# Row-wise dot products with a softmax on one core: another division of the last step, sums on ScalarE, and a later first store

## The chip, the cores and the metric

One core of one Trainium2 chip. The metric is the device time of a whole execution in microseconds (us); the span is the same execution from its first to its last instruction in the trace, some 1.8 us shorter. In the lines of the profile DVE is VectorE, ACT ScalarE, SP SyncE (which issues the loads); DVEq, ACTq and SPq are the sequencers of these engines.

## The reference

```python
def reference(x, y):                       # x, y: [8, 4096, 512] float32
    gram = np.matmul(x, y.transpose(0, 2, 1))
    diag = np.diagonal(gram, axis1=1, axis2=2)      # [8, 4096]: dot of row n of x with row n of y
    diag = diag - diag.max(axis=-1, keepdims=True)
    exp = np.exp(diag)
    return exp / exp.sum(axis=-1, keepdims=True)
```

Only the diagonal is needed: 32,768 dot products of 512 elements, then a softmax over each 4096. The inputs are 134 MB, the output 0.13 MB.

## The kernel before

The batches go in two sets of four. A set lies on 128 partitions (32 partitions for each batch), with 128 columns of dots for each partition. A set has four steps, and a step takes 32 rows for each partition: 8.39 MB of x and 8.39 MB of y. Six steps multiply the whole tile and reduce it. The last two use one combined multiply-and-sum (a "dot") for each row, and the last one is cut into pieces, so that little is left to do when the last bytes land.

```python
    # ... (views, pools, x in two tiles of 32 rows, y in one)
    def rows(t, r0, n):
        return xs[t % 2][:, r0 : r0 + n, :]

    def dots_of(t, r0, n):
        return diag[t * R // C][:, columns(t, r0, n)]

    def load_x(t, r0, n):
        nc.sync.dma_start(out=rows(t, r0, n), in_=xv[t * R // C, :, columns(t, r0, n), :])

    def load_y(t, r0, n):
        nc.sync.dma_start(out=ys[:, r0 : r0 + n, :], in_=yv[t * R // C, :, columns(t, r0, n), :])

    # ... products: xt = xt * yt on VectorE; sums: a reduce over the columns

    def dots(t, r0, n):
        for r in range(r0, r0 + n):
            xt = xs[t % 2][:, r, :]
            nc.vector.scalar_tensor_tensor(
                out=xt, in0=xt, scalar=1.0, in1=ys[:, r, :], op0=Alu.mult, op1=Alu.mult,
                accum_out=dots_of(t, r, 1),
            )

    # ... over_quadrant: reduces a [P, 1] column over its 32 partitions; largest: maximum over columns

    def exps(i, d):
        mxp = small.tile([P, 1], f32, name=f"mxp{i}")
        largest(mxp, d)
        nmx = over_quadrant(f"nmx{i}", mxp, Alu.max, negate=True)
        sump = small.tile([P, 1], f32, name=f"sump{i}")
        nc.scalar.activation(out=res[i], in_=diag[i][:, :C], func=Act.Exp, bias=nmx, scale=1.0, accum_out=sump)
        return sump

    def store(i, sump, n):
        total = over_quadrant(f"sum{i}", sump, Alu.add)
        rc = small.tile([P, 1], f32, name=f"rc{i}")
        nc.vector.reciprocal(out=rc, in_=total)
        nc.vector.tensor_single_scalar(out=res[i], in_=res[i], scalar=rc, op=Alu.mult)
        for p in range(0, P, n):
            nc.scalar.dma_start(out=ov[i, p : p + n, :], in_=res[i][p : p + n, :])

    for t in range(S - 2):
        load_x(t, 0, R)
        load_y(t, 0, R)
        nc.scalar.activation(out=side, in_=ys[:, R - K :, :], func=Act.Copy)
        products(t, 0, R - K, ys[:, : R - K, :])
        if t == C // R:
            store(0, sump, G)
        products(t, R - K, K, side)
        sums(t, 0, R)
        if t == C // R - 1:
            sump = exps(0, diag[0])

    t = S - 2
    load_x(t, 0, R)
    for r0 in (0, H):
        load_y(t, r0, H)
        dots(t, r0, H)

    t += 1
    r0 = 0
    for n in (16, 8, 4, 2, 1, 1):
        load_x(t, r0, n)
        load_y(t, r0, n)
        if r0 == 0:
            largest(diag[1][:, C : C + 1], diag[1][:, : C - R])
        if r0 == R - 2:
            largest(diag[1][:, C + 1 :], diag[1][:, C - R : C - 2])
        dots(t, r0, n)
        r0 += n
    store(1, exps(1, diag[1][:, C - 2 :]), P)
```

## Time and profile before

| | kernel before |
|---|---|
| time, median of the first 3 runs | 321.35 us (321.05 to 321.68) |
| span of the profiled run | 319.5 us |
| first load issued, last load landed | 0.73, 314.52 us |
| tail's maximum starts, last store issued | 315.35, 317.08 us |
| VectorE, ScalarE busy | 249.1, 18.9 us |

How to read it: the load stream fills the DMA engines from the start to about 313.4 us (busy share 9 tenths or more in 39 of 40 slices of the profile; 385 GB/s from 312 to 313 us, 150 in the microsecond after it and none from 314 to 315). What remains is a short stretch in which VectorE catches up with the last rows, and a serial tail (maximum, exchange over the quadrant, that is the 32 partitions of a batch, exponential, sum, reciprocal, scaling, store). The change works on these last 25 us, apart from the first set's store, which it takes out of the middle. The prediction below shows the lines.

The *first piece's start* is the start of the first VectorE multiplication of the last step. The *tail's maximum* is the first operation of the serial tail, the one whose output the program calls mxp.

### The profile page before, as it was taken

Reading aid. Unit: us, or ns where it says so; the run is one execution under the profiler, and the core shown is the slowest. Engines: PE = TensorE matmul, PEld = TensorE weight load, DVE = VectorE, ACT = ScalarE, POOL = GpSimd, SP = SyncE. Lnnn points to the kernel's source line nnn. Section 1 sums busy time; section 2 is a strip of 40 time slices with the busy share of each in tenths; the row PEclk is TensorE's granted clock in tenths of the full one; section 3 lists DMA queues with packets and bytes.
Section 4 is the critical chain, followed back from the end, with each engine's and each line's share of the span. In section 5 each row is a group of like instructions: output and inputs, shape, how many; then the busy total and the mean of one; then the engine's idle time right before and its main releaser. Section 6 shows DMA issues by size and latency. Waiting matters only on the chain.

```text
span 319.5 us, 284 instructions
## 1 busy us (share of the span) xinstructions
DVE 249.1 (78%) x158; ACT 18.9 (6%) x11; POOL 0.2 (0%) x4
## 2 busy tenths in 40 slices
DVE  0000079996899949999499995999959999994995
ACT  1000030000300003000120003000030000000000
POOL 0000000000000000000000000000000000000000
DMA  9999999999999999999999999999999999999992
GB/s 394 394 394 517 402 394 484 435 394 468 435 410 394 492 427 394 484 435 394 435 476 402 394 509 410 394 492 429 396 414 484 390 419 447 415 431 410 424 411 101
DMA packets 4225, 134.36 MB, mean 421 GB/s; under 512 B 512, under 2 KB 768, under 8 KB 1536
## 3 DMA queue, kind: packets, MB, share of 16 engines
q1 hardware_dynamic: 3888, 134.22, 97.6%
q10 hardware_dynamic: 336, 0.13, 0.1%
q14 instruction: 1, 0.01, 0.0%
HBM read 134.22 MB, written 0.13 MB: 421 GB/s over the span
## 4 chain that ended last, share of the span: by engine, by line
DMA 60%; DVE 36%; issue 2%; SPq 0%; ACT 0%; DVEq 0%
DMA ys<-in_y_dram 60%; DVE xs L69 27%; DVE xs L77 5%; DVE diag L72 4%; SPq L62 0%; DVE res L105 0%; DVE sum L85 0%; DVE nmx L85 0%; ACT res L98 0%; DVE rc L104 0%; DVE mxp L91 0%; SPq L65 0%; DVEq L69 0%; DVEq L77 0%
## 5 line engine op out<-in xcount | busy, mean ns | idle before, releaser
L69 DVE TENSOR_TENSOR xs<-xs,ys 128x13312 f32<-128x13312 f32 x6 | 84.2, 14025 | 62.3 <-DMA ys<-in_y_dram 62.3
L72 DVE TENSOR_REDUCE diag<-xs 128x32 f32<-128x16384 f32 x6 | 103.3, 17220 | 0.2
L77 DVE SCALAR_TENSOR_TENSOR xs<-xs,ys 128x512 f32<-128x512 f32 x64 | 39.6, 685 | 4.6 <-DMA ys<-in_y_dram 4.5
L112 ACT ACTIVATE side<-ys 128x3072 f32<-128x3072 f32 x6 | 16.6, 2765 | 187.5 <-DMA ys<-in_y_dram 151.4
L69 DVE TENSOR_TENSOR xs<-xs,side 128x3072 f32<-128x3072 f32 x6 | 20.1, 3351 | 0.0
L98 ACT ACTIVATE res<-diag,nmx 128x128 f32<-128x128 f32 x2 | 0.8, 402 | 109.2 <-DVE nmx L85 109.2
L77 DVE DVE_READ_ACCUMULATOR xs<-xs,ys 128x1 f32 x64 | 5.2, 81 | 0.0
L112 ACT ACT_TABLE_LOAD x1 | 1.3, 1283 | 0.7 <-PEq L153 0.7
L85 DVE TRANSPOSE_TENSOR_REDUCE sum<-sump 128x1 f32<-128x32 f32 x2 | 0.4, 208 | 0.6 <-ACT res L98 0.6
L105 DVE TENSOR_SCALAR res<-res,rc 128x128 f32<-128x128 f32 x2 | 0.6, 287 | 0.1
L91 DVE TENSOR_REDUCE mxp<-diag 128x1 f32<-128x128 f32 (+1 forms) x2 | 0.4, 222 | 0.1
L91 DVE TENSOR_REDUCE diag<-diag 128x1 f32<-128x96 f32 (+1 forms) x2 | 0.4, 218 | 0.1
L85 DVE TRANSPOSE_TENSOR_REDUCE nmx<-mxp 128x1 f32<-128x32 f32 x2 | 0.4, 212 | 0.1
L104 DVE RECIPROCAL rc<-sum 128x1 f32<-128x1 f32 x2 | 0.3, 164 | 0.1
L98 ACT ACTIVATION_READ_ACCUMULATOR res<-diag,nmx 128x1 f32 x2 | 0.4, 187 | 0.0
L153 POOL MEMSET const-uint8-127<- 128x1 uint8 x1 | 0.1, 103 | 0.0
L153 POOL MEMSET const-bfloat16-1.0<- 128x1 bf16 x1 | 0.1, 102 | 0.0
L153 POOL MEMSET const-float32-0.0<- 128x1 f32 x1 | 0.1, 99 | 0.2 <-issue 0.2
L153 POOL MEMSET const-float32-1.0<- 128x1 f32 x1 | 0.1, 99 | 0.0
## 6 DMA issues: line engine op xcount, KB each, us to landing
ys<-in_y_dram SPq DMA_DIRECT2D x3, 4096.0 KB, 14.9
xs<-in_x_dram SPq DMA_DIRECT2D x1, 4096.0 KB, 14.1
xs<-in_x_dram SPq DMA_DIRECT2D x1, 2048.0 KB, 18.5
ys<-in_y_dram SPq DMA_DIRECT2D x1, 2048.0 KB, 18.9
xs<-in_x_dram SPq DMA_DIRECT2D x1, 1024.0 KB, 21.0
ys<-in_y_dram SPq DMA_DIRECT2D x1, 1024.0 KB, 21.4
xs<-in_x_dram SPq DMA_DIRECT2D x1, 512.0 KB, 22.3
ys<-in_y_dram SPq DMA_DIRECT2D x1, 512.0 KB, 22.8
```

Of the source, the lines that this page charges most:

```text
L69: nc.vector.tensor_tensor(out=xt, in0=xt, in1=yt, op=Alu.mult)
L72: nc.vector.tensor_reduce(out=dots_of(t, r0, n), in_=rows(t, r0, n), axis=X, op=Alu.add)
L77: nc.vector.scalar_tensor_tensor(out=xt, in0=xt, scalar=1.0, in1=ys[:, r, :], op0=Alu.mult, op1=Alu.mult, accum_out=dots_of(t, r, 1),)
L85: nc.vector.tensor_reduce(out=got, in_=column.to_broadcast([P, G]), axis=X, op=op, negate=negate, apply_transpose=True)
L91: nc.vector.tensor_reduce(out=out, in_=d, axis=X, op=Alu.max)
L98: nc.scalar.activation(out=res[i], in_=diag[i][:, :C], func=Act.Exp, bias=nmx, scale=1.0, accum_out=sump)
L104: nc.vector.reciprocal(out=rc, in_=total)
L105: nc.vector.tensor_single_scalar(out=res[i], in_=res[i], scalar=rc, op=Alu.mult)
L112: nc.scalar.activation(out=side, in_=ys[:, R - K :, :], func=Act.Copy)
L153: nc = _bacc.Bacc("TRN2", target_bir_lowering=False, num_devices=1)
```

## The change

The intent is fourfold. The last row is split into two column halves, so that only half a dot follows the last landing. ScalarE sums 12 rows of the first piece, to unload VectorE. The first piece becomes one row larger and the last whole piece two rows. The store of the first set moves from the middle of the load stream to behind the last load.

```diff
 
 
@@ -58,11 +59,11 @@
     def dots_of(t, r0, n):
         return diag[t * R // C][:, columns(t, r0, n)]
 
-    def load_x(t, r0, n):
-        nc.sync.dma_start(out=rows(t, r0, n), in_=xv[t * R // C, :, columns(t, r0, n), :])
+    def load_x(t, r0, n, d=slice(0, D)):
+        nc.sync.dma_start(out=rows(t, r0, n)[:, :, d], in_=xv[t * R // C, :, columns(t, r0, n), d])
 
-    def load_y(t, r0, n):
-        nc.sync.dma_start(out=ys[:, r0 : r0 + n, :], in_=yv[t * R // C, :, columns(t, r0, n), :])
+    def load_y(t, r0, n, d=slice(0, D)):
+        nc.sync.dma_start(out=ys[:, r0 : r0 + n, d], in_=yv[t * R // C, :, columns(t, r0, n), d])
 
     def products(t, r0, n, yt):
         xt = rows(t, r0, n)
@@ -70,6 +71,11 @@
 
     def sums(t, r0, n):
         nc.vector.tensor_reduce(out=dots_of(t, r0, n), in_=rows(t, r0, n), axis=X, op=Alu.add)
+
+    def sums_act(t, r0, n):
+        for r in range(r0, r0 + n):
+            row = xs[t % 2][:, r, :]
+            nc.scalar.activation(out=row, in_=row, func=Act.Copy, accum_out=dots_of(t, r, 1))
 
     def dots(t, r0, n):
         for r in range(r0, r0 + n):
@@ -98,13 +104,11 @@
         nc.scalar.activation(out=res[i], in_=diag[i][:, :C], func=Act.Exp, bias=nmx, scale=1.0, accum_out=sump)
         return sump
 
-    def store(i, sump, n):
+    def normalize(i, sump):
         total = over_quadrant(f"sum{i}", sump, Alu.add)
         rc = small.tile([P, 1], f32, name=f"rc{i}")
         nc.vector.reciprocal(out=rc, in_=total)
         nc.vector.tensor_single_scalar(out=res[i], in_=res[i], scalar=rc, op=Alu.mult)
-        for p in range(0, P, n):
-            nc.scalar.dma_start(out=ov[i, p : p + n, :], in_=res[i][p : p + n, :])
 
     for t in range(S - 2):
         load_x(t, 0, R)
@@ -112,7 +116,7 @@
         nc.scalar.activation(out=side, in_=ys[:, R - K :, :], func=Act.Copy)
         products(t, 0, R - K, ys[:, : R - K, :])
         if t == C // R:
-            store(0, sump, G)
+            normalize(0, sump)
         products(t, R - K, K, side)
         sums(t, 0, R)
         if t == C // R - 1:
@@ -125,17 +129,39 @@
         dots(t, r0, H)
 
     t += 1
+    largest(diag[1][:, C : C + 1], diag[1][:, : C - R])
     r0 = 0
-    for n in (16, 8, 4, 2, 1, 1):
+    for n in (17, 8, 4, 2):
         load_x(t, r0, n)
         load_y(t, r0, n)
         if r0 == 0:
-            largest(diag[1][:, C : C + 1], diag[1][:, : C - R])
-        if r0 == R - 2:
-            largest(diag[1][:, C + 1 :], diag[1][:, C - R : C - 2])
-        dots(t, r0, n)
+            for r in (0, W // 2):
+                products(t, r, W // 2, ys[:, r : r + W // 2, :])
+                sums_act(t, r, W // 2)
+            dots(t, W, n - W)
+        else:
+            dots(t, r0, n)
         r0 += n
-    store(1, exps(1, diag[1][:, C - 2 :]), P)
+
+    left, right = slice(0, D // 2), slice(D // 2, D)
+    for d in (left, right):
+        load_x(t, r0, 1, d)
+        load_y(t, r0, 1, d)
+
+    for p in range(0, P, G):
+        nc.sync.dma_start(out=ov[0, p : p + G, :], in_=res[0][p : p + G, :])
+    largest(diag[1][:, C + 1 :], diag[1][:, C - R : C - 1])
+    part = small.tile([P, 1], f32, name="part")
+    xt, yt = xs[t % 2][:, r0, :], ys[:, r0, :]
+    nc.vector.scalar_tensor_tensor(
+        out=xt[:, left], in0=xt[:, left], scalar=1.0, in1=yt[:, left], op0=Alu.mult, op1=Alu.mult, accum_out=part
+    )
+    nc.vector.tensor_tensor_reduce(
+        out=xt[:, right], in0=xt[:, right], in1=yt[:, right], scale=1.0, scalar=part,
+        op0=Alu.mult, op1=Alu.add, accum_out=dots_of(t, r0, 1),
+    )
+    normalize(1, exps(1, diag[1][:, C - 1 :]))
+    nc.scalar.dma_start(out=ov[1], in_=res[1])
 
 
 # ---- launch: one core; inputs and outputs as the reference has them ----
```

More of the change, by code (lines that the diff above doesn't have):

```diff
@@ L32 @@
     K = 6
+    W = 12
     S = B // Q * (C // R)
```

## The prediction

Sum: -0.15 (earlier landings) + 0.06 (the smaller loads of the last row) - 0.27 (the last dot halved) + 0.4 (VectorE behind), which I put at -0.1 and so at 321.2 us. The term of 0.06: the 314.43 for the right half's landing contains it (314.52 - 0.15 + 0.06). The half dot's 0.42 us: the groups give the same as an estimate; 3351 ns for 3072 elements (a product) and 685 for 512 (a dot) differ by 1.04 ns an element, so 685 - 256 x 1.04 = 419 ns for 256.

> **What bounds the kernel now.** I read the page first (slices and DMA), then the chain that ended last, then the timeline of the last 30 us, then windows of 1 us over the last transfers, and last the groups for durations.
>
> ```profile
> DMA  9999999999999999999999999999999999999992
> GB/s 394 394 394 517 402 394 484 435 394 468 435 410 394 492 427 394 484 435 394 435 476 402 394 509 410 394 492 429 396 414 484 390 419 447 415 431 410 424 411 101
> HBM read 134.22 MB, written 0.13 MB: 421 GB/s over the span
> ```
> The DMA engines are busy in 39 of 40 slices; only the last one is empty. Single slices of GB/s jump; the mean counts.
>
> ```profile
> 80.90 14.04 DVE xs L69
> ...
> 197.33 14.04 DVE xs L69
> ...
> 304.44 10.09 DMA ys<-in_y_dram
> 314.52 0.03 issue
> ...
> 314.62 0.71 DVE xs L77 x2
> ...
> 315.35 0.17 DVE mxp L91
> ...
> 316.76 0.29 DVE res L105
> ```
> This is the chain of waits. Each big step starts when the last half of y has landed. From 80.90 to 197.33 lie three steps, 116.43 us; a step reads two tiles of 128 x 32 x 512 fp32, 16.78 MB, so 3 x 16.78 / 116.43 = 432 GB/s. The same rate holds to the end: seven steps of 16.78 MB from the first landing at 42.1 to the last at 314.5 make 117.44 / 272.4 = 431 GB/s. So the kernel is bound by the load stream up to 314.52, and then by a serial tail of 5.0 us up to the span's end at 319.5: last dot, maximum, exponential, sum, scaling, store.
>
> ```profile
> 294.69 0.69 DVE L77 SCALAR_TENSOR_TENSOR xs<-xs,ys 128x512 f32<-128x512 f32 x1 [4.06 <-DMA ys<-in_y_dram]
> 304.44 0.33 SPq L65 DMA_DIRECT2D ys<-in_y_dram  x1
> 312.02 0.69 DVE L77 SCALAR_TENSOR_TENSOR xs<-xs,ys 128x512 f32<-128x512 f32 x1
> 312.63 0.69 DVE L77 SCALAR_TENSOR_TENSOR xs<-xs,ys 128x512 f32<-128x512 f32 x1
> 313.36 0.18 DVE L91 TENSOR_REDUCE diag<-diag 128x1 f32<-128x30 f32 x1
> 313.47 0.68 DVE L77 SCALAR_TENSOR_TENSOR xs<-xs,ys 128x512 f32<-128x512 f32 x1
> 314.62 0.69 DVE L77 SCALAR_TENSOR_TENSOR xs<-xs,ys 128x512 f32<-128x512 f32 x1 [0.46 <-DMA ys<-in_y_dram]
> 317.08 0.36 ACTq L107 DMA_DIRECT2D out_dram<-res  x1
> ```
> The timeline of the last step. The first 16 rows of y have landed at 294.66. The very last load is issued at 304.44, just when the 8-row piece of y lands (the waits of the load queue put 12.4 us in three waits of this kind down to earlier loads: the ninth load after another waits for it, so about eight may be open). The eight rows behind that land by 314.52: 10.08 us for 4.19 MB, 416 GB/s or 1.26 us a row pair (x and y). One dot follows another every 0.613 us. VectorE waits 0.46 us before the last dot, so the landing sets the end, but by less than half a microsecond.
>
> ```profile
> 309.00:310.00 1.00, 1.00 (x3) 0.00 (x0) 0.00 (x0) 1.00 1.04 418
> 312.00:313.00 1.00, 0.98 (x3) 0.00 (x0) 0.00 (x0) 1.00 1.05 385
> 313.00:314.00 1.00, 0.97 (x4) 0.00 (x0) 0.00 (x0) 1.00 0.40 150
> 314.00:315.00 1.00, 0.54 (x3) 0.00 (x0) 0.00 (x0) 1.00 0.00 0
> ```
> The windows (last two columns: DMA share, GB/s). Bytes stop moving at about 313.4, so 1.1 us pass before the last landing is seen at 314.52. The single rows of 2 KB per partition run at 385 GB/s with full engines.
>
> ```profile
> L77 DVE SCALAR_TENSOR_TENSOR xs<-xs,ys 128x512 f32<-128x512 f32 x64 | 39.6, 685 | 4.6 <-DMA ys<-in_y_dram 4.5
> L112 ACT ACTIVATE side<-ys 128x3072 f32<-128x3072 f32 x6 | 16.6, 2765 | 187.5 <-DMA ys<-in_y_dram 151.4
> L69 DVE TENSOR_TENSOR xs<-xs,side 128x3072 f32<-128x3072 f32 x6 | 20.1, 3351 | 0.0
> ```
> The groups give the durations that I use below.
>
> [...]
>
> **The change part by part.**
>
> 1. *First set stored later.* Four stores (64 KB in all) leave the middle of the load stream and go behind the last load. At 432 GB/s 64 KB are 0.15 us, so every landing after them comes 0.15 us earlier. At the end they run in the empty engines after 313.4, while the tail of 5 us goes on; in the trace a 64 KB store landed 1.6 us after its issue. They should land by about 316, before the last store is even issued. Worth -0.15 on the landings, 0 at the end. ScalarE also gets rid of 1.8 us of issuing, which nobody waits for.
>
> 2. *17 rows in the first piece.* It lands one row pair later: 294.66 + 1.21 (0.524 MB at 432) - 0.15 = 295.72. VectorE then does two products of 6 rows (start to start 3.27: 3.35 less the 0.08 by which back-to-back products overlap in the timeline) = 6.54, and 5 dots = 3.07: 295.75 + 9.61 = 305.36. With 17 dots it would be 10.42, so the summing on ScalarE takes 0.81 us off VectorE.[...] Nobody needs these dots before 314.
>
> 3. *The next pieces.* y of the 8 rows lands at 304.40 + 1.21 - 0.15 = 305.46, so the 9.61 us above just fit. 4 rows later, at 1.26 a row: 310.50; 2 rows later: 313.02. VectorE: 8 dots 305.5 to 310.4, 4 dots 310.55 to 313.0, 2 dots 313.1 to 314.35 with the accumulator. It keeps pace with the loads and no more; both clocks agree within 0.15 us.
>
> 4. *The last row.* Loads: a row pair in four transfers with 1 KB runs.[...] VectorE meanwhile: the maximum over 31 columns goes ahead of the halves (0.11 start to start in the trace): left half from 314.47. [...]with its accumulator it ends at about 314.9. The right half takes the left sum as its starting value, so it can't overlap: 0.04 us of gap as between the reciprocal and the scaling that uses it, then 0.42, end 315.35 if its accumulator is a separate 0.08, 315.27 if not. Now the right half's landing at 314.43 is hidden by 0.4 us.
>
> 5. *The tail from the maximum on*: same instructions, same sizes (3 columns in place of 4). Before, it starts at 315.35. In the changed kernel at 315.30 to 315.40 by the VectorE chain. No more lies between it and the end.
>
> Sum: landings earlier by 0.15[...], last dot halved (-0.27), but VectorE behind by 0.4 because it now has 2 dots, a maximum and two chained halves after the landing at 313.02: -0.1 with what the steps leave open (about 0.15 either way). Span 319.4, time 321.35 - 0.15 = **321.2 us**.
>
> **The rivals.** *A, VectorE keeps up better than I think* (the 0.42 overlaps, the combined multiply-and-sum has no separate accumulator read): then the landing at 314.43 sets the end, right half 314.5 to 314.95, 0.4 us saved: 320.9. For it: VectorE was idle 0.46 us there before. Against: its work after the 2-row landing is 1.23 + 0.11 + 0.9 us, longer than the 1.4 us to the last landing. *B, the first set's stores end last*: they wait for earlier loads to land before they are issued, like the loads of row 30 and 31 that the queue held back for 4.5 us each. The fourth store waits for the 2-row y at 313.0 and is issued by 313.4, so it should land by about 316; were it to delay the last store, it would cost up to about 1 us: 322.2. Against: engines are at 0.00 share from 314 on. *C, the combined operation is dear*: no trace here has it. If it took 1 us in place of 0.42, the end would be 0.6 later: 321.8. *D, VectorE slips in the first piece*: were the two products slowed or the ScalarE sums in its way by 0.5 us, all of that lands at the end, since the pieces leave no slack: 321.8.
>
> **Range and chances.** A change of 2% is 6.4 us, and the whole tail plus all loss of the stream is 5.0 + about 2; nothing in the change touches more than 1 us of it. The three runs before spread over 0.6 us. Range 320.6 to 321.7, between rival A with some luck and C or D. Faster by over 2%: 0.01; within: 0.97; slower: 0.02, for something like a start-up cost of the new operation that no trace shows.
>
> **What would show it.** Step 1: the two steps after 197.33 are shorter by about 0.15 us in all, and no DMA work after 316 but the last store. Step 2: first dot-like work at about 295.7, ScalarE sums done before 310. Step 3: waits on y before the pieces of 8, 4 and 2 rows under 0.2 us. Step 4: no wait on y before the right half, and the maximum of the tail at 315.2 to 315.4. Wrong, if the right half waits on a load (then A, or the 1 KB loads are slow), if the chain ends with the first set's stores (B), or if the combined operation takes over 0.6 us (C).

## The result

| | before | changed |
|---|---|---|
| median (same chip, 6 runs each) | 321.58 us (321.05 to 321.89) | 322.16 us (321.48 to 322.90) |
| ratio | 1 | 1.0018 (1.0002 to 1.0035) |
| span of the profiled run | 319.5 | 320.2 |
| first piece's start | 294.69 | 296.14 |
| tail's maximum starts | 315.35 | 316.06 |
| last store issued | 317.08 | 317.85 |

The time lies above the range of 320.6 to 321.7.

The timeline of the changed kernel, its last step (start, duration, engine, line, operation; in brackets the idle time ahead and what ended it):

```profile
296.14 6.63 DVE L70 TENSOR_TENSOR xs<-xs,ys 128x3072 f32<-128x3072 f32 x2 [5.61 <-DMA ys<-in_y_dram]
...
306.00 0.69 DVE L83 SCALAR_TENSOR_TENSOR xs<-xs,ys 128x512 f32<-128x512 f32 x1 [0.17 <-DMA ys<-in_y_dram]
...
313.55 0.69 DVE L83 SCALAR_TENSOR_TENSOR xs<-xs,ys 128x512 f32<-128x512 f32 x1
...
314.78 0.08 DVE L83 DVE_READ_ACCUMULATOR xs<-xs,ys 128x1 f32 x1
314.96 0.18 DVE L97 TENSOR_REDUCE diag<-diag 128x1 f32<-128x31 f32 x1
315.07 0.43 DVE L156 SCALAR_TENSOR_TENSOR xs<-xs,ys 128x256 f32<-128x256 f32 x1
...
315.54 0.48 DVE L159 CUSTOM_DVE_ANT_0 xs<-xs,ys,part 128x256 f32<-128x256 f32 x1
...
316.06 0.16 DVE L97 TENSOR_REDUCE mxp<-diag 128x1 f32<-128x3 f32 x1
```

Before the last dot there used to be a wait of 0.46 us for the last load. Here nothing waits for a load after the start of the two dots at 313.55. That start is still set by a landing: the fourth store of the first set waits for the y of the 2-row piece to land, and is issued at 313.47, 0.08 us before it.

```profile
313.47 0.31 SPq L152 DMA_DIRECT2D out_dram<-res  x1
```

From there VectorE works through two dots, a maximum and two halves, one behind the other, for 2.51 us, and the loads of the last row have landed somewhere under this work. The new combined operation (the custom one) takes 0.48 us.

The chain of waits of the changed kernel at the same place (start, length, what):

```profile
313.55 1.32 DVE xs L83 x4
...
314.90 0.02 DVEq L97
314.92 0.04 issue
314.96 0.06 DVE diag L97
...
316.26 0.22 DVE nmx L91
...
316.50 0.02 ACTq L104
316.52 0.04 issue
316.56 0.07 ACT res L104
```

In the kernel before, this chain came to its last dot from a load of 10.09 us. Here it stays on VectorE to the end. Two entries are new: DVEq ahead of the maximum and ACTq ahead of the exponential, a sequencer step of 0.02 us with 0.02 to 0.04 on either side. b3 below returns to them.

The windows of 1 us at the end of the changed kernel (last two columns: DMA share, GB/s):

```profile
312.00:313.00 1.00, 1.00 (x5) 0.00 (x0) 0.00 (x0) 1.00 1.06 353
313.00:314.00 1.00, 0.96 (x3) 0.00 (x0) 0.00 (x0) 1.00 0.56 176
314.00:315.00 1.00, 0.90 (x5) 0.00 (x0) 0.00 (x0) 1.00 0.13 33
```

Bytes move a little longer than before (33 GB/s after 314, where there was nothing): the first set's stores, probably. They are over by 315 (0 GB/s from 314.6 on). Two of the four stores are issued well before the loads have come to rest: at 308.40 and 310.89, the last one at 313.47. From the last store's issue to the span's end it is 2.35 us, against 2.42 before.

The group lines of ScalarE's new work and of the two halves (count, busy us, mean ns, idle time ahead):

```profile
L78 ACT ACTIVATE xs<-xs 128x512 f32<-128x512 f32 x12 | 7.4, 615 | 60.7 <-DVE xs L70 60.7
L78 ACT ACTIVATION_READ_ACCUMULATOR xs<-xs 128x1 f32 x12 | 2.2, 187 | 0.0
L156 DVE SCALAR_TENSOR_TENSOR xs<-xs,ys 128x256 f32<-128x256 f32 x1 | 0.4, 426 | 0.0
L159 DVE CUSTOM_DVE_ANT_0 xs<-xs,ys,part 128x256 f32<-128x256 f32 x1 | 0.5, 485 | 0.0
```

The duration that the prediction took for the plain half (0.42) holds (426 ns), and so does the 6.54 us for the two products of 6 rows (296.14 to 302.68, where the first dot behind them starts). ScalarE's sums follow each other every 0.61 us, the accumulator read of 187 ns lying beside the sum before and the one after it, and end at 307.0: early enough.

### The profile page after: what moved, and what is told of

It is laid out like the page before. It is cut to its first block, busy times and chain, and to the rows that moved or that the text cites. A ratio compares the mean times of both kernels' runs of the same rounds, so it can differ in the third digit from the quotient of the medians.

```text
span 320.2 us, 288 instructions
## 1 busy us (share of the span) xinstructions
DVE 248.6 (78%) x138; ACT 26.3 (8%) x35; POOL 0.2 (0%) x4
## 4 chain that ended last, share of the span: by engine, by line
DMA 57%; DVE 39%; issue 2%; SPq 0%; ACT 0%; DVEq 0%; ACTq 0%
DMA ys<-in_y_dram 57%; DVE xs L70 27%; DVE xs L83 8%; DVE diag L73 4%; DVE xs L159 0%; SPq L63 0%; DVE res L111 0%; ACT res L104 0%; DVE sum L91 0%; DVE nmx L91 0%; DVE xs L156 0%; DVE rc L110 0%; DVE mxp L97 0%; DVEq L70 0%; SPq L66 0%
## 5 line engine op out<-in xcount | busy, mean ns | idle before, releaser
L70 DVE TENSOR_TENSOR xs<-xs,ys 128x13312 f32<-128x13312 f32 (+1 forms) x8 | 90.8, 11357 | 67.8 <-DMA ys<-in_y_dram 67.8
L83 DVE SCALAR_TENSOR_TENSOR xs<-xs,ys 128x512 f32<-128x512 f32 x51 | 31.6, 685 | 0.2 <-DMA ys<-in_y_dram 0.2
L70 DVE TENSOR_TENSOR xs<-xs,side 128x3072 f32<-128x3072 f32 x6 | 20.1, 3351 | 0.0
L78 ACT ACTIVATE xs<-xs 128x512 f32<-128x512 f32 x12 | 7.4, 615 | 60.7 <-DVE xs L70 60.7
L83 DVE DVE_READ_ACCUMULATOR xs<-xs,ys 128x1 f32 x51 | 4.1, 81 | 0.0
L78 ACT ACTIVATION_READ_ACCUMULATOR xs<-xs 128x1 f32 x12 | 2.2, 187 | 0.0
## 6 DMA issues: line engine op xcount, KB each, us to landing
ys<-in_y_dram SPq DMA_DIRECT2D x2, 4096.0 KB, 20.3
```

Source lines behind the costliest of these rows:

```text
L70: nc.vector.tensor_tensor(out=xt, in0=xt, in1=yt, op=Alu.mult)
L78: nc.scalar.activation(out=row, in_=row, func=Act.Copy, accum_out=dots_of(t, r, 1))
L83: nc.vector.scalar_tensor_tensor(out=xt, in0=xt, scalar=1.0, in1=ys[:, r, :], op0=Alu.mult, op1=Alu.mult, accum_out=dots_of(t, r, 1),)
```

## The experiments

The theory after the result (theory 1): behind the landing of the 2-row piece VectorE has more serial work (2.51 us) than the rest of the stream takes, so halving the last row saves nothing, and the end comes later than before. Its rivals: the moved stores or the 1 KB loads spoil the landings or the end (theory 2), and the load stream itself is some tenths of a microsecond earlier or later from run to run (theory 3).

Times of 0.1 to 0.3% are at the edge of what the runs resolve. So each experiment is judged by its trace as well, by a figure that a late stream doesn't move: **the time from the first piece's start to the tail's maximum**. A kernel with a 17-row first piece starts it one row pair later than one with 16 rows: 1.21 us by its bytes at 432 GB/s, and up to 1.36 by the landings told at the end. So to be compared with a 16-row kernel a 17-row kernel's figure needs 1.21 to 1.36 us more.

| run | pieces of the last step | median us (before, same chip) | ratio (95%) | first piece's start | tail's maximum | difference |
|---|---|---|---|---|---|---|
| before, first profile | 16,8,4,2,1,1 | 321.35 | | 294.69 | 315.35 | 20.66 |
| a1 before again | 16,8,4,2,1,1 | 321.82 (321.31) | 1.0018 (1.0005 to 1.0032) | 294.74 | 315.43 | 20.69 |
| changed, first profile | 17,8,4,2, halves | 322.16 (321.58) | 1.0018 (1.0002 to 1.0035) | 296.14 | 316.06 | 19.92 |
| a2 changed again | 17,8,4,2, halves | 321.92 (321.31) | 1.0021 (1.0009 to 1.0033) | 296.21 | 316.12 | 19.91 |
| a3 last row whole | 17,8,4,2,1 | 321.71 (321.31) | 1.0008 (0.9996 to 1.0020) | 296.00 | 315.63 | 19.63 |
| a4 first set in the middle | 17,8,4,2, halves | 322.26 (321.31) | 1.0030 (1.0018 to 1.0042) | 296.01 | 315.85 | 19.84 |
| b1 before, stored late | 16,8,4,2,1,1 | 321.67 (321.26) | 1.0009 (0.9994 to 1.0024) | 294.55 | 315.27 | 20.72 |
| b2 before, halves | 16,8,4,2,1, halves | 321.34 (321.26) | 1.0009 (0.9989 to 1.0030) | 294.79 | 315.35 | 20.56 |
| b3 no ScalarE sums | 17,8,4,2, halves | 322.17 (321.26) | 1.0026 (1.0010 to 1.0042) | 295.54 | 315.74 | 20.20 |
| b4 row 30 alone | 16,8,4,2,1, halves | 321.87 (321.26) | 1.0020 (0.9995 to 1.0045) | 295.61 | 316.29 | 20.68 |
| c1 six-row piece | 17,8,6, halves | 324.95 (321.50) | 1.0105 (1.0085 to 1.0125) | 297.56 | 319.78 | 22.22 |
| c2 changed again | 17,8,4,2, halves | 321.89 (321.50) | 1.0014 (0.9995 to 1.0034) | 295.97 | 315.88 | 19.91 |
| c3 row 30 alone, again | 16,8,4,2,1, halves | 321.71 (321.50) | 1.0002 (0.9986 to 1.0019) | 294.91 | 315.63 | 20.72 |
| c4 early shift | 16,8,4,2,1, halves | 321.64 (321.50) | 0.9990 (0.9970 to 1.0010) | 296.04 | (none) | |

### a1: the kernel before against itself

No edit but a comment.

> A null test: the kernel before against itself. If runs scatter as they did (321.05 to 321.89 us), the ratio is 1.000 with an interval of about 0.15% either way. It also gives a second profile of the landings: in the first, y of the second-last step's first half landed at 265.15 us, the 16-row piece of y at 294.66 and the last load at 314.52. Theory 1 (the end is late because VectorE has too much to do after the 2-row piece has landed) needs these to repeat within 0.2 us in every kernel; theory 3 (the stream itself lands up to 0.5 us earlier or later from run to run) expects them to differ by 0.3 us or more.

The timeline of this second profile of the kernel before:

```profile
294.74 0.69 DVE L77 SCALAR_TENSOR_TENSOR xs<-xs,ys 128x512 f32<-128x512 f32 x1 [4.25 <-DMA ys<-in_y_dram]
...
314.70 0.69 DVE L77 SCALAR_TENSOR_TENSOR xs<-xs,ys 128x512 f32<-128x512 f32 x1 [0.47 <-DMA ys<-in_y_dram]
...
315.43 0.16 DVE L91 TENSOR_REDUCE mxp<-diag 128x1 f32<-128x4 f32 x1
```

The profile repeats within 0.08 us, wait and all. The time doesn't: three of the six runs took 321.2 to 321.4 us and three 322.2 to 322.6, and the ratio of the kernel to itself is 1.0018, with an interval that excludes 1. So the expectation of 1.000 missed, and it follows that the timed ratio of the change, also 1.0018, could by itself come from the scatter of runs. Whether the change costs anything has to be read from the traces, or from an experiment with a larger effect.

### a2 and c2: the changed kernel again

No edit but a comment.

> The changed kernel once more. Theory 1: 1.001 to 1.003 of before again, the 2-row piece of y lands within 0.2 us of 313.45 and 2.5 us pass from the start of the two dots to the tail's maximum. Theory 3 (stream jitter made the profiled run late): the landing of the first half of y in the second-last step, 265.8 in the profile of the changed kernel against 265.15 before, comes back to about 265.2, with all later landings 0.5 us earlier, and the ratio falls to about 1.000.

> The changed kernel a third time, for its time on this chip beside the other two: 321.8 to 322.3 us. Where its profile falls in an undisturbed run (y of the second-last step 19.6 us after its issue in the median, x of that step 23.0), the tail's maximum starts at 315.7 to 315.9, still 0.4 us later than in the kernel before, and 19.9 us after the first piece's start. If the lateness was the stream's alone, it starts at 315.4.

In three profiles, taken at three different times, the first piece starts at 295.97 to 296.21 and the tail's maximum follows 19.91 to 19.92 us later. With 1.21 to 1.36 us for the 17th row that is 21.1 to 21.3 us, against 20.66 and 20.69 for the kernel before: the structure is 0.4 to 0.6 us longer, the same each time. That is theory 1's part. But the run of a2 was not free of theory 3: the loads of y in the second-last step took 20.3 us in the median to land, as in the first profile of the changed kernel, where both profiles of the kernel before have 19.6. c2 had 20.3 as well, so the comparison that I had set for it (an undisturbed run) did not come about. But a4 below supplies it but for the place of the stores: its y and x took 19.6 and 23.0 us, as in both profiles of the kernel before, and its tail's maximum still started at 315.85, 0.42 and 0.50 us later than theirs. So a late stream alone doesn't explain the changed kernel.

### a3: the last row whole

```diff
-    left, right = slice(0, D // 2), slice(D // 2, D)
-    for d in (left, right):
-        load_x(t, r0, 1, d)
-        load_y(t, r0, 1, d)
+    load_x(t, r0, 1)
+    load_y(t, r0, 1)
     ...   # stores of the first set and the maximum over 31 columns stay here
-    (the two chained halves)
+    dots(t, r0, 1)
```

> The changed kernel with its last row loaded and multiplied whole (17, 8, 4, 2, 1), the maximum over 31 columns still before it. Theory 1: after the 2-row landing VectorE does two dots (1.31), the maximum (0.12 to 0.2) and one dot (0.7), together about 2.15 to 2.25 us up to the tail's maximum in place of 2.51, so it is 0.25 to 0.3 us faster than the changed kernel: halving the last row costs time, as nothing waits for its loads. Theory 2 (1 KB loads land late): faster by the lateness of the landing, with no wait on loads before the last dot in either. If halving helped as meant, this is slower than the changed kernel by 0.2 to 0.3 us.

```profile
296.00 6.63 DVE L70 TENSOR_TENSOR xs<-xs,ys 128x3072 f32<-128x3072 f32 x2 [5.42 <-DMA ys<-in_y_dram]
...
313.38 0.69 DVE L83 SCALAR_TENSOR_TENSOR xs<-xs,ys 128x512 f32<-128x512 f32 x1
...
314.79 0.18 DVE L97 TENSOR_REDUCE diag<-diag 128x1 f32<-128x31 f32 x1
314.90 0.69 DVE L83 SCALAR_TENSOR_TENSOR xs<-xs,ys 128x512 f32<-128x512 f32 x1
...
315.63 0.16 DVE L97 TENSOR_REDUCE mxp<-diag 128x1 f32<-128x3 f32 x1
```

From the two dots to the tail's maximum it is 2.25 us in place of 2.51, and from the first piece's start 19.63 in place of 19.91. So without its halves the kernel is 0.26 to 0.28 us shorter, as expected; and the last dot still starts without a wait for a load. In this design halving the last row only adds an instruction to the engine that is behind. The times agree in direction (1.0008 against 1.0021 in the same rounds), which scatter alone could give.

### a4: the first set stored in the middle again

```diff
             normalize(0, sump)
+            for p in range(0, P, G):
+                nc.scalar.dma_start(out=ov[0, p : p + G, :], in_=res[0][p : p + G, :])
     ...
-    for p in range(0, P, G):
-        nc.sync.dma_start(out=ov[0, p : p + G, :], in_=res[0][p : p + G, :])
```

> The changed kernel with the first set stored in the middle again, from ScalarE. My prediction says the 64 KB cost the load stream 0.15 us, so this is 0.15 us slower than the changed kernel. Theory 2b (stores behind the last load hold the end back, through their queue or their landing): faster than the changed kernel by 0.2 us or more, with a shorter time from the last store's issue (317.85) to the span's end (320.2), now 2.35 us. Theory 1: no difference beyond 0.15 us.

```profile
296.01 3.36 DVE L70 TENSOR_TENSOR xs<-xs,ys 128x3072 f32<-128x3072 f32 x1 [5.49 <-DMA ys<-in_y_dram]
...
315.85 0.16 DVE L97 TENSOR_REDUCE mxp<-diag 128x1 f32<-128x3 f32 x1
```

19.84 us from start to maximum, within 0.1 of the changed kernel: the moved stores don't make the end late, and theory 2b falls. The span's end comes 2.36 us after the last store's issue (317.64 to 320.0), as in the changed kernel. The median is 0.34 us above that of a2, in the direction of my 0.15; given a1, that is no proof.

### b1: the kernel before, with its first set stored late

```diff
     def store(i, sump, n):
         ...
-        for p in range(0, P, n):
-            nc.scalar.dma_start(out=ov[i, p : p + n, :], in_=res[i][p : p + n, :])
+        if i:
+            nc.scalar.dma_start(out=ov[i], in_=res[i])
     ...                                     # in the last step, behind the last load:
+        if r0 == R - 1:
+            for p in range(0, P, G):
+                nc.sync.dma_start(out=ov[0, p : p + G, :], in_=res[0][p : p + G, :])
```

> The kernel before with one part of the change: its first set stored behind the last load. If the 64 KB are taken out of the stream, the second-last step's y lands 0.15 us earlier and the tail's maximum starts 0.15 us earlier than 315.35 to 315.43 in the profiles of the kernel before, and the stores end under the tail: 321.2 us, a ratio of 0.9995. If the gain is eaten by the waits further on (in the profile of the changed kernel with the first set in the middle the landings at the end were no later), there is no difference. If stores hold up the end, it is 0.2 us or more slower, and the span's end is over 2.45 us after the last store's issue. The timed ratio can't settle this, as the kernel before against itself gave 1.0018; the profile can.

The tail's maximum starts at 315.27, 0.08 to 0.16 us earlier than in the two profiles of the kernel before, and the last store is issued at 317.00, 2.4 us before the end. That is the size that I had expected, in a single profile. Where it comes from can be seen in the chain of waits. The line of the step that had the stores, of the kernel before:

```profile
211.42 24.69 DMA ys<-in_y_dram
```

of this one:

```profile
211.29 24.52 DMA ys<-in_y_dram
```

The load of y lands 0.17 us sooner after its issue: 64 KB at 432 GB/s are 0.15. All four kernels with the stores in the middle have 24.69 to 24.71 here, and nine of ten with late stores 24.51 to 24.60 (the first profile of the changed kernel has 24.85). So this gain is there, in this step.

### b2: the kernel before, with halves

```diff
-    for n in (16, 8, 4, 2, 1, 1):
+    for n in (16, 8, 4, 2, 1):
     ...
+    (the loads of the two column halves and the two chained operations, as in the change)
```

> The kernel before with one part of the change: the last row in two column halves with chained dots, row 30 still a piece of its own. Theory 1: here VectorE has only one dot and the left half to do after row 30 has landed, so it does wait for the right half; the tail's maximum starts about 0.55 to 0.6 us after the last landing in place of 0.83, so at 315.1 to 315.25 against 315.35 to 315.43. If the 1 KB loads are slow (theory 2), the last landing comes later than 314.5 to 314.6 and eats it.

```profile
294.79 0.69 DVE L77 SCALAR_TENSOR_TENSOR xs<-xs,ys 128x512 f32<-128x512 f32 x1 [4.15 <-DMA ys<-in_y_dram]
...
314.15 0.42 DVE L144 SCALAR_TENSOR_TENSOR xs<-xs,ys 128x256 f32<-128x256 f32 x1
314.82 0.48 DVE L147 CUSTOM_DVE_ANT_0 xs<-xs,ys,part 128x256 f32<-128x256 f32 x1 [0.24 <-DVE xs L144]
315.35 0.16 DVE L91 TENSOR_REDUCE mxp<-diag 128x1 f32<-128x4 f32 x1
```

20.56 us in place of 20.66 and 20.69. So the halves are worth 0.1 us where VectorE does wait for the last load, and the 0.23 to 0.28 that I had expected (0.55 to 0.6 us behind the last landing in place of 0.83) was too much. The wait of 0.24 us is put down to the left half on VectorE itself, but this had ended at 314.57; the chain of waits has the load of the right half of y landing at 314.59, so it was the load. That is 19.80 us after the first piece's start, where the last whole row landed 19.83 and 19.86 us after it in the two profiles of the kernel before: the 1 KB loads are not late, and this part of theory 2 falls. Between the landing and the maximum lie 0.76 us here and 0.83 with a whole row: the custom operation starts later after its landing (0.23 here, 0.16 in c3, against 0.10 for a plain dot) and takes 0.06 us more than the plain half.

### b3: no sums on ScalarE

```diff
-            for r in (0, W // 2):
-                products(t, r, W // 2, ys[:, r : r + W // 2, :])
-                sums_act(t, r, W // 2)
-            dots(t, W, n - W)
+            dots(t, 0, n)
```

> The changed kernel with all 17 rows of its first piece as dots on VectorE. Theory 1: VectorE then finishes the first piece at about 306.6 in place of 305.8, is behind the landings from there on, and all pieces run back to back: tail's maximum at 296.1 + 17 x 0.613 + 14 x 0.613 + 1.3 = about 316.5, that is 0.4 to 0.6 us later than in the changed kernel (316.06, 316.12); 322.4 to 322.7 us. If VectorE's load in the first piece doesn't matter (the loads set every start), no difference.

```profile
295.54 0.69 DVE L83 SCALAR_TENSOR_TENSOR xs<-xs,ys 128x512 f32<-128x512 f32 x1 [5.30 <-DMA ys<-in_y_dram]
...
314.53 0.08 DVE L83 DVE_READ_ACCUMULATOR xs<-xs,ys 128x1 f32 x1
314.65 0.18 DVE L97 TENSOR_REDUCE diag<-diag 128x1 f32<-128x31 f32 x1
...
315.93 0.21 DVE L91 TRANSPOSE_TENSOR_REDUCE nmx<-mxp 128x1 f32<-128x32 f32 x1
316.18 0.40 ACT L104 ACTIVATE res<-diag,nmx 128x128 f32<-128x128 f32 x1 [77.61 <-DVE nmx L91]
```

All 31 dots run back to back, with no wait for a load in between, and the maximum comes 20.20 us after the start: 0.29 us more than in the changed kernel, where I had expected 0.4 to 0.6 (and 316.5 where 315.74 came, as the stream of this run was also half a microsecond early). So ScalarE's help is worth 0.3 us in this division, not the 0.81 us that it takes off VectorE's load: in the changed kernel the landings set the starts of the next pieces (gaps of 0.26, 0.07 and 0.13 us against dots back to back), and its maximum over 31 columns starts 0.06 us later for another reason, which follows.

This run also explains the two new entries of the chain. From the last accumulator's end (314.61) to the maximum over 31 columns are 0.04 us here, and 0.10 in the changed kernel (314.86 to 314.96); from the quadrant's maximum to the exponential 0.04 here (316.14 to 316.18) and 0.09 there. The two operations read columns which, in the changed kernel, come from ScalarE as well as from VectorE, and there the chain shows the sequencer step DVEq or ACTq in front of each. ScalarE was done at 307.0, so the data were not late. That this step is the wait for the second engine is my reading of the chain; that the gap is 0.05 to 0.06 us longer each time, and shrinks again when ScalarE's sums go, is shown.

### c1: the suspected cost made larger

```diff
-    for n in (17, 8, 4, 2):
+    for n in (17, 8, 6):
```

> The changed kernel with the suspected cost made larger: pieces of 17, 8 and 6 rows in place of 17, 8, 4 and 2, then the same halves; same bytes, same operations. The 6 rows land when the 2-row piece landed (17.35 us after the 17 rows). Theory 1 (VectorE's serial work after the last whole piece sets the end): 6 dots in place of 2 come after it, 4 x 0.613 = 2.45 us more, tail's maximum 22.4 us after the first piece's start in place of 19.9; about 324.4 us, a ratio near 1.009 to 1.010. If the landings set the end, no difference.

```profile
297.56 6.63 DVE L70 TENSOR_TENSOR xs<-xs,ys 128x3072 f32<-128x3072 f32 x2 [7.09 <-DMA ys<-in_y_dram]
...
314.81 0.69 DVE L83 SCALAR_TENSOR_TENSOR xs<-xs,ys 128x512 f32<-128x512 f32 x1 [2.41 <-DMA ys<-in_y_dram]
...
319.25 0.48 DVE L159 CUSTOM_DVE_ANT_0 xs<-xs,ys,part 128x256 f32<-128x256 f32 x1
...
319.78 0.16 DVE L97 TENSOR_REDUCE mxp<-diag 128x1 f32<-128x3 f32 x1
```

Same bytes and the same operations, with four more dots behind the last landing of a whole piece. The difference grows from 19.91 to 22.22, by 2.31 us (expected 2.45), and the time by 3.06 us against the changed kernel in the same rounds (324.95 against 321.89), a ratio of 1.0105 to the kernel before. VectorE idles 2.41 us ahead of the six rows, and never after. Here the effect is well clear of the scatter: in this kernel the length of VectorE's work after the last whole piece sets the end. (The trace accounts for 2.31 of the 3.06 us. Its own run was the slowest of six, with a first piece 1.59 us after that of c2; I put the rest down to such late streams, which is not shown. Between the lowest runs, 324.43 and 321.80, the difference is 2.63 us.)

### b4 and c3: row 30 a piece of its own

Row 30, counted from 0, is the second-last of the step's 32 rows.

```diff
-    for n in (17, 8, 4, 2):
+    for n in (16, 8, 4, 2, 1):
     ...
         else:
+            if r0 == R - 2:
+                largest(diag[1][:, C + 1 :], diag[1][:, C - R : C - 2])
             dots(t, r0, n)
     ...
-    largest(diag[1][:, C + 1 :], diag[1][:, C - R : C - 1])
     ...
-    normalize(1, exps(1, diag[1][:, C - 1 :]))
+    normalize(1, exps(1, diag[1][:, C - 2 :]))
```

> The changed kernel with the pieces 16, 8, 4, 2, 1 and then the halves, the maximum over the columns so far ahead of row 30 as in the kernel before; ScalarE sums, the late stores and the chained halves stay. Theory 1: row 30 lands at about 313.2, its dot ends by 314.0, VectorE waits for the right half (314.4 to 314.6) and the tail's maximum starts at 315.0 to 315.2, 0.9 us earlier than in the changed kernel and 0.2 to 0.3 us earlier than in the kernel before: a ratio of 0.998 to 1.000 on this chip. If the lateness comes from the halves, the stores or the ScalarE sums themselves, it stays as late as the changed kernel, 315.9 or more.

> The kernel with 16, 8, 4, 2, 1 rows and the halves once more, as its first profile fell in a run in which the stream was 0.8 us late from the second-last step on. In an undisturbed run: the 16 rows start at 294.6 to 294.8, the tail's maximum 20.6 us later at 315.2 to 315.4. Theory 1: 0.5 us faster than the changed kernel in the same rounds; the lowest run within 0.1 us of the lowest of the kernel before (321.1).

The profile of b4 fell in a run whose first piece started 0.9 us late, at 295.61; c3 repeats it. Of c3:

```profile
294.91 6.63 DVE L70 TENSOR_TENSOR xs<-xs,ys 128x3072 f32<-128x3072 f32 x2 [4.05 <-DMA ys<-in_y_dram]
...
314.46 0.42 DVE L157 SCALAR_TENSOR_TENSOR xs<-xs,ys 128x256 f32<-128x256 f32 x1
315.10 0.49 DVE L160 CUSTOM_DVE_ANT_0 xs<-xs,ys,part 128x256 f32<-128x256 f32 x1 [0.22 <-DMA ys<-in_y_dram]
315.63 0.16 DVE L97 TENSOR_REDUCE mxp<-diag 128x1 f32<-128x4 f32 x1
```

Late stores, ScalarE sums and chained halves are all still there; only the order of the last three rows' work differs. VectorE waits for the right half again (0.22 us), and the difference is 20.68 and 20.72, against 21.1 to 21.3 for the changed kernel: 0.4 to 0.6 us are back. So late stores, ScalarE sums and halves do not make it late by themselves; what went with the lateness is that two dots, the maximum and the halves stand behind one landing. The edit also goes back from 17 to 16 rows in the first piece, and no run takes that back alone; the 1.21 to 1.36 us added for the 17th row are part of the comparison. A count that needs no such addition, from the landing of the step ahead (in the chain of waits) to the tail's maximum, agrees: 79.24 and 79.46 us in the kernel before, 80.02 to 80.05 in the three profiles of the changed kernel, 79.86 in a4, 79.29 in c3 (80.06 in b4, with its late stream).

It is no better than the kernel before (20.66, 20.69), where I had expected 0.2 to 0.3 us. b2 tells part of it: the halves are worth 0.1 us there. And the right half landed 20.03 us after the start in c3 (314.94) and 19.99 in b4, 0.2 us later than the 19.80 of b2, which takes that 0.1 away. The smaller loads are the same in all three, so they are not the reason. What differs is ScalarE's sums and the late stores, of which c3 issues the first at 310.95, before the last loads have landed; that the stores take their 64 KB from the last loads is a guess of mine that no run tested alone. In time, c3 is 0.18 us below c2 and not 0.5; the lowest runs are 321.49 and 321.80, and the expected lowest run near 321.1 did not come. With this scatter neither is a proof.

### c4: an earlier shift

On top of c3, the exponential's shift (the maximum that is subtracted) comes from the first 96 columns, found while VectorE waits for the last step:

```diff
-    largest(diag[1][:, C : C + 1], diag[1][:, : C - R])
+    mxp = small.tile([P, 1], f32, name="mxp1")
+    largest(mxp, diag[1][:, : C - R])
+    nmx = over_quadrant("nmx1", mxp, Alu.max, negate=True)
     ...   # no maximum over the last 32 columns, and none in the tail
-    normalize(1, exps(1, diag[1][:, C - 2 :]))
+    sump = small.tile([P, 1], f32, name="sump1")
+    nc.scalar.activation(out=res[1], in_=diag[1][:, :C], func=Act.Exp, bias=nmx, scale=1.0, accum_out=sump)
+    normalize(1, sump)
```

> As the run with row 30 alone, and the exponential's shift taken from the maximum of the first 96 columns, found while VectorE waits for the last step, so that the maximum and its exchange over the quadrant (0.19 + 0.25 us) leave the serial tail.[...] Expected: 0.44 us off the tail, time from the last multiply to the last store's issue 1.3 us in place of 1.75 to 1.8; lowest run about 320.65, median 0.4 us below the run with row 30 alone, 320.9 to 321.2; faster than the kernel before by 0.1%.

```profile
296.04 6.63 DVE L70 TENSOR_TENSOR xs<-xs,ys 128x3072 f32<-128x3072 f32 x2 [5.45 <-DMA ys<-in_y_dram]
...
316.55 0.08 DVE L160 DVE_READ_ACCUMULATOR2_ANT diag<- 128x1 f32 x1
316.73 0.40 ACT L165 ACTIVATE res<-diag,nmx 128x128 f32<-128x128 f32 x1 [9.84 <-DVE diag L160]
...
318.02 0.37 ACTq L167 DMA_DIRECT2D out_dram<-res  x1
```

From the first piece's start to the last store's issue it is 21.98 us, against 22.51 in c3 (294.91 to 317.42) and 22.39 in the kernel before (294.69 to 317.08). So the tail is 0.4 us shorter than the kernel before's in this count, about the 0.44 that was expected. The lowest run, 320.74, is the lowest of all runs. But this run's stream was late (the first piece starts at 296.04, 1.1 us after that of c3), and over six runs the ratio is 0.999 (0.997 to 1.001): not resolved. The result was correct on these inputs; it needs no dot of the last 32 rows to lie so far above the maximum of the others that the exponential leaves the range of the number type (how far was not tried), which the kernel before doesn't need. So no version has been shown to beat the kernel before in time.

## Why the prediction was wrong

Step by step, against the profile of the changed kernel. The tail's maximum was predicted for 315.30 to 315.40 and started at 316.06: 0.71 us late. The span's end, predicted for 319.4, came at 320.2. The mechanism stood: VectorE keeps pace with the landings, the right half's landing is hidden, and the tail follows. Two terms of the sum failed: the landing of the first piece (step 2), 0.39 us too early, and VectorE's chain from there to the tail's maximum (steps 3 and 4), 0.32 us too short.

- **Step 2, the first piece's landing: 0.39 us (296.14 for 295.75).** This is the larger of the two terms; why it is that large is only in part known. It has three parts.
  - The 17th row was put at 1.21 us, its bytes at 432 GB/s. From the landing of the step ahead (in the chain of waits) to the first piece's start, five of the seven profiles with 16 rows have 58.57 to 58.77 us, and six of the seven with 17 rows 59.82 to 60.13 (left out are b4, c4 and c1, where the stream lost 0.7 us or more on the way). The means, 58.67 and 60.03, differ by 1.36; the three 17-row profiles whose second-last step landed soonest (a3, a4, b3) have a mean of 59.93 and a difference of 1.26. So 0.05 to 0.15 us.
  - The late stores were to bring all landings 0.15 us forward. They did so in their own step (0.17, see b1), but this did not reach the last step whole: the step ahead of the first piece landed at 235.99 on average over ten profiles with late stores, and at 236.04 over four with the stores in the middle; and in eight of those ten the second-last step's loads of y took longer (20.0 to 21.3 us in the median, against 19.6 to 19.7 in all four with the stores in the middle). So of the 0.15 us about 0.05 arrived at that step, and perhaps nothing at the last one.
  - The rest I put down to scatter of the stream from run to run. In the three profiles of this kernel the landing came 0.22 to 0.46 us late; whether the moved stores have a part in that stays open.
- **Steps 3 and 4, VectorE's chain: 0.32 us (19.92 us from start to maximum for 19.60).** The terms of the sum that were mis-sized are: the work up to the start of the two dots 0.06 (17.41 for 17.35), from the dots to the maximum over 31 columns 0.15 (1.41 for 1.26: 0.08 of it was a slip, as the kernel before shows 1.34 for the same work, 312.02 to 313.36, and 0.06 is the gap that b3 takes away), and from the combined operation's start to the tail's maximum 0.11 (0.52 for 0.41: 0.48 for the operation, not 0.42). Each is small, but nothing waited any more that could have absorbed them, and they added up.
- **The sum.** The prediction's own terms don't give its -0.1: -0.15 + 0.06 - 0.27 + 0.4 is +0.04, and its own start of the tail, 315.30 to 315.40, is that of the kernel before (315.35). Added up rightly it forecast no change, not 321.2 us (without the 0.06, -0.02). (A smaller slip: it is the eighth load behind another that waits for it, not the ninth: y of row 30 for y of the 16-row piece, issued and landed at 294.66.)
- **Step 4, the verdict on the halves.** I had them as a gain of 0.27 us that is then lost elsewhere. a3 shows that in this division they cost 0.26 to 0.28, and b2 that even where the load is waited for they bring 0.1. The 0.06 us that the sum had for the 1 KB loads isn't seen in b2: the last landing comes 19.80 us after the first piece's start, against 19.83 and 19.86 with a whole row.
- **Step 5, "same instructions, same sizes" in the tail:** 1.79 us from the maximum to the last store's issue in place of 1.73: the gap ahead of the exponential, 0.05, gone in b3 (1.73 there).
- **Step 1, stores under the tail:** right for the end: their bytes were over by 315, and the end follows the last store's issue by 2.35 us as before (a4, b1). But they don't wait for empty engines: the first is issued at 308.40, 5 us before the loads' bytes stop (c3 shows what that may cost).
- **The rivals:** A (VectorE keeps up better) was the wrong way round. B (stores end last) fell with a4 and b1. C (a dear combined operation) was right in direction and 0.06 us in size, not 0.6. D (VectorE slips in the first piece, all of it lands at the end) was right in what follows from a slip, but the slip was in the landing and in the last three rows.
- **The range** (320.6 to 321.7) took three runs of one program within 0.6 us for the scatter. The kernel before ran at 321.58 beside the change, 0.23 above the figure that I had started from, and a1 shows runs of the same program 1.4 us apart. With 0.7 us of lateness in the trace the range had no room.

What stays open: why a run's stream is up to 1.6 us late from the second-last step on; whether late stores make this more frequent (eight of ten profiles against none of four suggest it, but a1 and b2, with the stores in the middle, also have timed runs 1 us above their lowest); and how much of the timed 0.58 us is structure. The traces put the structure at 0.4 to 0.6 us. That work behind the last whole landing moves the end is confirmed clear of the scatter by c1; that it is what makes this change late, and by how much, stands in the traces alone (a3, a4, b4, c3).

## What to carry to other kernels

Halving the last operation gained 0.1 us where it waits for its load (b2, a wait of 0.24 us) and cost 0.26 to 0.28 where nothing is waited for (a3): look for the idle time in front of it, and make sure that the change leaves some. When the loads and an engine run at the same pace down to the last piece, as here, arrange the pieces so that the engine has as little as possible to do behind each of the last landings; merging pieces of 4 and 2 rows into one of 6 put four more dots behind the last whole landing and the tail's maximum 2.31 us later (c1). And time a kernel against itself before believing 0.2%: here the same program gave a ratio of 1.0018 (a1).
